# One step of a hybrid diffusion backbone: the values of four heads in one place, and when the output projection's buffers open

## The chip, the cores and the metric

The kernel runs on one core of a Trainium2 chip. The metric is the device time of one execution in microseconds, as the median of several runs. Names: PE is TensorE's matmuls and PEld its weight loads, DVE is VectorE, ACT ScalarE, POOL GpSimd, SP the engine whose queue issues the DMAs.

## The reference

Two identical layers. In each, one projection of the modulated input feeds four mixers; their gated outputs are joined and projected back, and a layer norm over the residual follows. The change touches mixer B (neighbourhood attention) and the output projection.

```
h   = x * (1 + scale) + shift
u   = h @ w_in + b_in
out = concat_g(mixer_g(u_g) * SiLU(gate_g)) @ w_out + b_out
x   = LayerNorm(alpha * x + gate * out)

# mixer B: 32 x 64 grid, 4 heads of 64; window of 8 rows x 16 columns, and all 256 context keys
s_loc = einsum('brchd,brjwhd->brhcjw', qg, kg) * scale
s_loc = where(col_in, s_loc + bias, NEG_INF)
s_ctx = einsum('brchd,bshd->brhcs', qg, k_ctx) * scale
p = softmax(concatenate([s_loc, s_ctx]))
o = einsum(p_loc, vg) + einsum(p_ctx, v_ctx)
```

There are 2048 latent tokens (32 rows of 64) and 128 context tokens of a new request, which attend only among themselves ("prompt" in the code). All is fp32; products that need it are split into a high and a low part and take three matmuls.

## The kernel before

Each layer has four stages: input projection, grouped-query attention, neighbourhood attention (phase3) and output projection (phase4). A stage opens pools of SBUF buffers on two stacks, one from the left and one from the right ("left" and "right" in `sub`), and closes them at its end. A buffer that comes to lie where an older one was can be written only when all readers of the old one are done, a DMA store among them. Order on each engine's queue is set by a planner, which takes instructions by readiness and program order; for this stage no order is written by hand. A queue runs strictly in the order that it was given.

**The neighbourhood attention** (L1213) works on 16 tiles, 8 groups i of four grid rows (in NAT_ORDER, 1 2 0 3 4 5 7 6) by two column halves e. Groups 0 and 7 are edge groups with a bias of their own, be, which a pool of one buffer holds in turn with the prompt's operands; the others use a resident bias bi. The loop at L1342 runs over pairs of heads, two steps a tile, as a pipeline of three: at step s the scores of pair s (L1266, L1267 into ps_d, two banks that phase 4 shares; then VectorE's L1272 adds the bias and takes the maximum, and ScalarE's L1276 the exponential), the transposes of pair s-1 (L1299; part 0 is copied to pT by VectorE at L1301, part 1 by ScalarE at L1303), and the values of pair s-2 (L1314, into ps_a, one bank; 5 key chunks a head in edge tiles and 6 in the others). With the second pair, `finish` broadcasts the denominators over TensorE (L1325), multiplies onto the gates gt (L1334) and, for e = 1, stores gt to the mixed output (L1337). pT has three buffers, one for each head in flight.

A value matmul has 64 output rows, so TensorE runs it in 128x64 form; scores, transposes and L1325 are in 128x128 form.

At step 8 `load_p4pre` fetches w_out in four chunks of 1 MB through the buffers of mx (two) and splits each: woh on ScalarE (L1453), wol on GpSimd (L1454). Steps 15 and 20 insert the prompt's attentions.

**The output projection** (L1464) takes 17 tiles t of 128 tokens. `load_mix(p)` loads two tiles' columns into mx, `prep(t)` (L1496) splits them into mhi (ScalarE, L1503, two halves) and mlo (GpSimd, L1507; for t = 0 VectorE makes the first half), in one set of buffers for even t and one for odd t (pmh). `main(t)` is 48 matmuls (L1536 to L1538, 2 column halves by 8 k by 3), its evacuation starts at L1529. Since open_p4pre opens the mx buffers and the even set before the attention runs, the planner may move load_mix and the first preps into the attention's last third, and it does.

Of the kernel before, what the change touches and what calls it, by code (L numbers as in the profile page):

```python
# [8 lines left out]
F32 = mybir.dt.float32  # L9
# [113 lines left out]
class Kern:  # L123
# [1081 lines left out]

    def phase3(self, l):
        P = lambda n, b: self.sub(f"p3{n}{l}", "p3", b, "right")
        self.open_p4pre(l)
        self.b2, self.be1 = P("b2", 2), P("be", 1)
        self._phase3(l)  # L1210
        self.close("p3")

    def _phase3(self, l):  # L1213
# [75 lines left out]
        def transp(i, e, h, part):  # L1289
            d = st[i, e]  # L1290
            p = d["p", h]
            ch = chunks(i, e)
            if part == 0:
                d["pT", h] = self.b3.tile([128, 6, 128], F32, tag="pT", name="pT")
            pT = d["pT", h]
            a, b = (0, len(ch) - 3) if part == 0 else (len(ch) - 3, len(ch))
            t = self.third((128, 4, 128))
            for c in range(a, b):
                nc.tensor.transpose(t[:, c - a, :], p[:, ch[c][0]:ch[c][0] + 128], self.id)  # L1299
            if part == 0:  # L1300
                nc.vector.tensor_copy(pT[:, a:b, :], t[:, :b - a, :])  # L1301
            else:
                nc.scalar.activation(pT[:, a:b, :], t[:, :b - a, :], AF.Copy)  # L1303
                d.pop(("p", h))

        def values(i, e, pr):
            d = st[i, e]
            if pr == 0:
                d["acc"] = self.bank("a", (128, 4, 128))
            ch = chunks(i, e)  # L1310
            for c, (_, vt, ti) in enumerate(ch):
                for hh in range(2):
                    h = pr * 2 + hh
                    nc.tensor.matmul(  # L1314
                        d["acc"][hh * 64:(hh + 1) * 64, pr, :], vt[:, ti, h * 64:(h + 1) * 64], d["pT", h][:, c, :],
                        start=(c == 0), stop=(c == len(ch) - 1),
                    )

        def finish(i, e):
            d = st.pop((i, e))  # L1320
            zb = self.b2.tile([128, 4, 64], F32, tag="zb", name="zb", bufs=1)
            nc.vector.reciprocal(d["z"], d["z"])
            nc.vector.tensor_copy(zb, d["z"].unsqueeze(2).to_broadcast([128, 4, 64]))
            for c in range(2):
                nc.tensor.matmul(  # L1325
                    d["acc"][:, 2 + c, :], zb[:, 2 * c:2 * c + 2, :].rearrange("p h d -> p (h d)"), self.id,
                    start=True, stop=True,
                )
            gt = gates[i]
            acc = d["acc"].rearrange("p a (r c) -> p a r c", r=4)  # L1330
            for x in (1, 0):
                for c in range(2):
                    g = gt[:, c, :].rearrange("p (r s c) -> p r s c", r=4, s=2)[:, :, e, :]
                    nc.vector.tensor_tensor(g, acc[:, 2 * x + c], g, op=ALU.mult)  # L1334
            if e == 1:
                c0 = NPR + i * 256
                nc.sync.dma_start(S["mix"][256:512, c0:c0 + 256].rearrange("(c p) t -> p c t", p=128), gates.pop(i))  # L1337
# [4 lines left out]
        for s in range(n + 2):  # L1342
            if s < n:
                i, e, pr = pairs[s]
                if pr == 0:
                    begin(i, e)
                scores(i, e, 2 * pr)
                scores(i, e, 2 * pr + 1)
                if pr == 1 and e == 1 and d_edge(i):
                    held.pop(("tile", i))  # L1350
                    load_edge()
            if 0 <= s - 1 < n:
                i, e, pr = pairs[s - 1]
                for hh in range(2):
                    transp(i, e, 2 * pr + hh, 0)
                    transp(i, e, 2 * pr + hh, 1)
            if 0 <= s - 2 < n:
                i, e, pr = pairs[s - 2]
                values(i, e, pr)
                if pr == 1:  # L1360
                    finish(i, e)
                    x = tiles.index((i, e))
                    if x + 2 < len(tiles):
                        self.load_nv(*tiles[x + 2])
            if s == 8:
                self.load_p4pre(l)
            if s in (15, 20):
                gqa = s == 20
                self.prompt_attn(l, gqa, *held.pop(("prompt", gqa)))
                load_edge()  # L1370
# [25 lines left out]
    def prompt_attn(self, l, gqa, q, k, v, gt):  # L1396

        nc, S = self.nc, self.S
        zb = self.b2.tile([128, 4, 64], F32, tag="zb", name="pzb", bufs=1)
        r0 = 768 if gqa else 256  # L1400
        s = self.bank("d", (128, 1024))
        for h in range(4):
            kh = h // 2 if gqa else h
            for i in range(2):
                nc.tensor.matmul(
                    s[:, h * 128:(h + 1) * 128], q[i][:, h, :].bitcast(F32R), k[:, kh, :].bitcast(F32R),
                    start=(i == 0), stop=(i == 1),
                )
        m = self.b2.tile([128, 8], F32, tag="pm", name="pm", bufs=1)
        s4 = s[:, 0:512].rearrange("p (h t) -> p h t", h=4)  # L1410
        nc.vector.tensor_reduce(m[:, 0:4], s4, axis=AX.X, op=ALU.max, negate=True)
        p = self.b3.tile([128, 4, 128], F32, tag="p", name="pp")
        z = m[:, 4:8]
        for h in range(4):
            nc.scalar.activation(p[:, h, :], s4[:, h, :], AF.Exp, bias=m[:, h:h + 1], accum_out=z[:, h:h + 1])
        t = self.third((128, 4, 128))
        for h in range(4):
            nc.tensor.transpose(t[:, h, :], p[:, h, :], self.id)
        pT = self.b3.tile([128, 4, 128], F32, tag="pT", name="ppT")
        nc.vector.tensor_copy(pT, t)  # L1420
        nc.vector.reciprocal(z, z)
        nc.vector.tensor_copy(zb, z.unsqueeze(2).to_broadcast([128, 4, 64]))
        acc = self.third((128, 4, 128))
        for h in range(4):
            kh = h // 2 if gqa else h
            nc.tensor.matmul(
                acc[(h % 2) * 64:(h % 2) * 64 + 64, h // 2, :], v[:, kh * 64:(kh + 1) * 64], pT[:, h, :],
                start=True, stop=True,
            )
        for c in range(2):  # L1430
            nc.tensor.matmul(
                acc[:, 2 + c, :], zb[:, 2 * c:2 * c + 2, :].rearrange("p h d -> p (h d)"), self.id, start=True, stop=True
            )
        nc.vector.tensor_tensor(gt, acc[:, 2:4, :], gt, op=ALU.mult)
        nc.vector.tensor_tensor(gt, acc[:, 0:2, :], gt, op=ALU.mult)
        nc.sync.dma_start(S["mix"][r0:r0 + 256, :NPR].rearrange("(c p) t -> p c t", p=128), gt)


    def open_p4pre(self, l):

        nc, A = self.nc, self.A
        c1 = self.sub(f"p4w{l}", "p4", 1, "left")
        self.pmx = self.sub(f"p4m{l}", "p4", 2, "left")
        self.pmh = [self.sub(f"p4h{l}", "p4", 1, "left"), None]
        self.woh = c1.tile([128, 8, 1024], F32R, name="woh")
        self.wol = c1.tile([128, 8, 1024], F32R, name="wol")

    def load_p4pre(self, l):
        nc, A = self.nc, self.A
        for k in range(0, 8, 2):  # L1450
            w = self.pmx.tile([128, 2, 1024], F32, tag="mx", name="wo")
            nc.sync.dma_start(w, A["w_out"][l][k * 128:(k + 2) * 128, :].rearrange("(k p) n -> p k n", p=128))
            nc.scalar.activation(self.woh[:, k:k + 2, :], w, AF.Copy)  # L1453
            nc.gpsimd.tensor_tensor(self.wol[:, k:k + 2, :], w, f32(self.woh[:, k:k + 2, :]), op=ALU.subtract)  # L1454

    def phase4(self, l):
        P = lambda n, b: self.sub(f"p4{n}{l}", "p4", b, "left")
        self.pmh[1], self.c1, self.b2 = P("h1", 1), P("c", 1), P("b2", 2)
        if l + 1 < self.depth:
            self.open_p1pre(l + 1)  # L1460
        self._phase4(l)
        self.close("p4")

    def _phase4(self, l):  # L1464
# [3 lines left out]
        mt = {}  # L1468

        def load_mix(p):  # L1470
            m = self.pmx.tile([128, 8, 256], F32, tag="mx", name="mx")
            n = min(256, T - p * 256)
            nc.sync.dma_start(m[:, :, :n], S["mix"][:, p * 256:p * 256 + n].rearrange("(k p) t -> p k t", p=128))
            mt[p] = m
# [262 lines left out]
```

## Time and profile before

| | us |
|---|---|
| median of 3 runs (lowest, highest) | 2886.11 (2882.16, 2894.56) |
| the profiled execution, its time | 2888.61 |
| its span from the first to the last instruction | 2886.7 |
| TensorE busy in the span | 2777.3 (96%) |
| VectorE busy | 1959.3 (68%) |
| GpSimd busy | 1100.5 (38%) |
| ScalarE busy | 1079.2 (37%) |
| mean granted TensorE clock | 0.984 |

Neighbourhood attention: about 1106 to 1287 us (layer 0) and 2526 to 2707 us (layer 1). Output projection: from there to 1495 and to the end; its first matmuls already run at 1266 and 2685.

How to read it: TensorE is busy nearly throughout, so shares of the whole span say little on a change in one stage. A table of busy times by stretch says which engine a stage is bound by; the waits name what an engine stood for; the timeline shows the queue around one wait. A busy TensorE includes the pitch that it loses at a change between forms. In a timeline row, equal instructions that follow one another are drawn together: start, time, engine, line, operation, operands, form, count, and in brackets the idle time before and what ended it.

### The profile page before, as it was taken

The numbers are of one execution on the slowest core, as the hardware profiler recorded it, in microseconds if no ns is written. First come the engines' busy times: TensorE is split into PE (matmuls) and PEld (weight loads), VectorE is DVE, ScalarE is ACT, GpSimd is POOL, SyncE is SP. The second block draws the span as 40 slices with busy tenths as digits, with TensorE's granted clock in tenths as the row PEclk, the third lists the DMA queues.
The fourth block names the chain that finished last, engine by engine and source line by source line (L and its number), as shares of the span: only waits on it lengthen the run. The fifth ranks groups of instructions, "written<-read, shape, count | busy, mean of one in ns | idle before, by whom it ended". The sixth has DMA issues, their size and how long they took to land. (4 is left out here: it accounts for less than half of the span.)

```text
span 2886.7 us, 45477 instructions
## 1 busy us (share of the span) xinstructions
PE 2777.3 (96%) x16960; PEld 2272.2 (79%) x16960; DVE 1959.3 (68%) x3503; ACT 1079.2 (37%) x1922; POOL 1100.5 (38%) x716
## 2 busy tenths in 40 slices
PE   7999999999999999999999899999999999999998
PEld 6988989999555556887779899999985555577887
DVE  2895246944478886749868963398436888676687
ACT  4233431333344445542222334313323444465210
POOL 3353420512466666014323534213215666730232
PEclk9999999999999999999999999999999999999999
DMA  9665775665361005646755556746555201076452
GB/s 311 216 209 185 212 251 178 194 201 158 89 146 35 21 21 155 166 137 225 235 180 176 175 182 189 239 149 219 148 157 121 71 24 35 8 206 177 135 168 103
DMA packets 384381, 447.80 MB, mean 155 GB/s; under 512 B 54432, under 2 KB 338592, under 8 KB 382368
## 3 DMA queue, kind: packets, MB, share of 16 engines
q1 hardware_dynamic: 384160, 444.89, 51.3%
q8 instruction: 134, 2.20, 0.3%
q14 instruction: 87, 0.71, 0.1%
HBM read 279.39 MB, written 165.39 MB: 154 GB/s over the span
## 5 line engine op out<-in xcount | busy, mean ns | idle before, releaser
L308 PE MATMUL ps_u<-hhi,whi 128*128 128x384 f32 (+1 forms) x1712 | 567.8, 335 | 11.0 <-ACT hhi L391 8.7
L309 PE MATMUL ps_u<-hlo,whi 128*128 128x384 f32 (+1 forms) x1712 | 567.2, 332 | 1.5 <-POOL hlo L393 0.7
L310 PE MATMUL ps_u<-hhi,wlo 128*128 128x384 f32 (+1 forms) x1712 | 565.8, 331 | 0.0
L1067 POOL TENSOR_TENSOR zp<-zp,e 128x1024 f32<-128x1024 f32 x160 | 388.5, 2428 | 217.7 <-ACT e L1049 214.1
L1049 ACT ACTIVATE e<-ps_d 128x1024 f32<-128x1024 f32 x288 | 292.0, 1024 | 361.1 <-PE ps_d L1047 328.7
L783 DVE SCALAR_TENSOR_TENSOR cacc<-cz,small,cacc 128x1166 f32<-128x1166 f32 (+1 forms) x240 | 356.7, 1486 | 3.5
L308 PEld LDWEIGHTS ps_u<-hhi,whi 128*128 128x128 f32 x1712 | 326.0, 191 | 20.3 <-ACT hhi L391 12.0
L309 PEld LDWEIGHTS ps_u<-hlo,whi 128*128 128x128 f32 x1712 | 326.9, 191 | 6.0 <-POOL hlo L393 2.6
L310 PEld LDWEIGHTS ps_u<-hhi,wlo 128*128 128x128 f32 x1712 | 326.7, 191 | 1.8 <-issue 1.0
L970 DVE TENSOR_REDUCE mx<-ps_s 128x1 f32<-128x512 f32 (+1 forms) x374 | 228.5, 631 | 122.1 <-PE ps_s L967 117.9
L1055 PE MATMUL ps_a<-e,gvv 128*64 128x512 f32 x1152 | 281.2, 609 | 0.0
L1507 POOL TENSOR_TENSOR mlo<-mx,mhi 128x512 fp32r<-128x512 f32 x66 | 110.8, 1698 | 417.4 <-ACT mhi L1503 417.4
L308 PE MATMUL ps_u<-whi,hhi 128*128 128x256 f32 x816 | 236.1, 289 | 0.0
L309 PE MATMUL ps_u<-wlo,hhi 128*128 128x256 f32 x816 | 234.9, 288 | 0.0
L310 PE MATMUL ps_u<-whi,hlo 128*128 128x256 f32 x816 | 234.8, 288 | 0.0
L433 POOL TENSOR_TENSOR wlo<-ws,whi 128x512 fp32r<-128x512 f32 x92 | 142.5, 1558 | 202.7 <-ACT whi L432 190.4
L1536 PE MATMUL ps_d<-woh,mhi 128*128 128x512 f32 x512 | 200.9, 392 | 0.0
L1537 PE MATMUL ps_d<-wol,mhi 128*128 128x512 f32 x512 | 200.7, 392 | 0.0
L1538 PE MATMUL ps_d<-woh,mlo 128*128 128x512 f32 x512 | 200.4, 391 | 0.0
L1029 PE MATMUL ps_d<-q,k 128*128 128x512 f32 x576 | 187.0, 407 | 2.6 <-ACT e L1049 2.0
L1047 PE MATMUL ps_d<-q,k 65*128 65x512 f32 x560 | 178.3, 399 | 0.2 <-ACT q L980 0.2
L1055 PEld LDWEIGHTS ps_a<-e,gvv 128*64 128x64 f32 x1152 | 71.7, 137 | 127.3 <-issue 125.0
(285 smaller groups left out, 5475.5 us busy)
## 6 DMA issues: line engine op xcount, KB each, us to landing
ws<-in_w_in SPq DMA_DIRECT2D x80, 256.0 KB
mw<-in_w_mod SPq DMA_DIRECT2D x32, 512.0 KB
nq<-s_nq SPq DMA_DIRECT2D x64, 256.0 KB
mx<-s_mix SPq DMA_DIRECT2D x16, 1024.0 KB
s_gate<-ev SPq DMA_DIRECT2D x80, 192.0 KB
s_qh<-qT SPq DMA_DIRECT2D x34, 256.0 KB
x<-in_x SPq DMA_DIRECT2D x17, 512.0 KB
s_xT<-xo SPq DMA_DIRECT2D x17, 512.0 KB
```

Source lines behind the costliest of these rows:

```text
L308: mm(p, ah, bh, start=(k == 0), stop=False)
L309: mm(p, ah, bl, start=False, stop=False)
L310: return mm(p, al, bh, start=False, stop=(k == 7))
L783: nc.vector.scalar_tensor_tensor(acc[:, c, :n], z[:, k:k + n], cw[:, c, k:k + 1], acc[:, c, :n], op0=ALU.mult, op1=ALU.add)
L970: r = nc.vector.tensor_reduce(mx[:, h, i:i + 1], p[:, :n], axis=AX.X, op=ALU.max)
L1029: nc.tensor.matmul(s[:, kv * 512:(kv + 1) * 512], k1[kv][:, j * 128:(j + 1) * 128], q1[:, 2 * kv:2 * kv + 2, :].rearrange("p h t -> p (h t ...
L1049: nc.scalar.activation(e, s, AF.Exp)
L1055: nc.tensor.matmul(acc[kv * 64:(kv + 1) * 64, :], vv[:, j, kv * 64:(kv + 1) * 64], e[:, kv * 512:(kv + 1) * 512], start=(j == 0), stop=(j ...
L1067: nc.gpsimd.tensor_tensor(zp, zp, e, op=ALU.add)
L1536: nc.tensor.matmul(o, hi[:, k, :], woh[:, k, ns], start=(k == 0), stop=False)
L1537: nc.tensor.matmul(o, hi[:, k, :], wol[:, k, ns], start=False, stop=False)
L1538: nc.tensor.matmul(o, lo[:, k, :], woh[:, k, ns], start=False, stop=(k == 7))
```

## The change

Three edits. In the loop of the neighbourhood attention, `values` of both pairs of a tile is called at the second pair's step, so that of the first pair comes one step later. pT moves to a pool of its own with six buffers instead of three, opened ahead of the output projection's early buffers. And these early buffers shrink to the weights and one mx buffer, through which w_out is loaded; the second mx buffer and the even mhi/mlo set are opened with phase 4, on top of the left-hand stack, at the addresses they had.

```diff
@@ phase3
         P = lambda n, b: self.sub(f"p3{n}{l}", "p3", b, "right")
+        self.b3t = P("t", 6)
         self.open_p4pre(l)
@@ transp, and likewise ppT in prompt_attn
-                d["pT", h] = self.b3.tile([128, 6, 128], F32, tag="pT", name="pT")
+                d["pT", h] = self.b3t.tile([128, 6, 128], F32, tag="pT", name="pT")
@@ _phase3, the loop
                 i, e, pr = pairs[s - 2]
-                values(i, e, pr)
                 if pr == 1:
+
+                    values(i, e, 0)
+                    values(i, e, 1)
                     finish(i, e)
@@ open_p4pre
-        self.pmx = self.sub(f"p4m{l}", "p4", 2, "left")
-        self.pmh = [self.sub(f"p4h{l}", "p4", 1, "left"), None]
+        self.pmx = [self.sub(f"p4m{l}", "p4", 1, "left")]
@@ load_p4pre
-            w = self.pmx.tile([128, 2, 1024], F32, tag="mx", name="wo")
+            w = self.pmx[0].tile([128, 2, 1024], F32, tag="mx", name="wo")
@@ phase4
-        self.pmh[1], self.c1, self.b2 = P("h1", 1), P("c", 1), P("b2", 2)
+        self.pmx.append(P("m1", 1))
+        self.pmh = [P("h", 1), P("h1", 1)]
+        self.c1, self.b2 = P("c", 1), P("b2", 2)
@@ load_mix
-            m = self.pmx.tile([128, 8, 256], F32, tag="mx", name="mx")
+            m = self.pmx[p % 2].tile([128, 8, 256], F32, tag="mx", name="mx")
```

## Rows read from the trace of the kernel before

**Rows 1.** Busy by stretch: PE, PEld, DVE, ACT, POOL, clock, DMA, GB/s.

```profile
1106.00:1287.00 181.00, 173.17 (x1539) 144.88 (x1538) 120.73 (x372) 100.19 (x220) 29.88 (x12) 0.99 0.61 167
1230.00:1240.00 10.00, 6.78 (x53) 6.04 (x52) 4.82 (x17) 5.63 (x13) 1.28 (x1) 0.83 1.11 282
2650.00:2660.00 10.00, 7.22 (x58) 6.04 (x59) 5.74 (x17) 5.29 (x12) 1.26 (x1) 0.83 1.02 252
1340.00:1370.00 30.00, 26.69 (x126) 21.77 (x125) 29.23 (x42) 10.93 (x22) 15.39 (x11) 1.00 0.71 227
2780.00:2820.00 40.00, 40.00 (x178) 33.14 (x177) 32.72 (x37) 5.80 (x12) 13.89 (x8) 1.00 0.47 158
```

**Rows 2.** Waits of PE, 1106 to 1287: total us, times, longest.

```profile
PE ps_d L1266 <- DVE m L1272: 4.4, 3, 3.2
```

**Rows 3.** Timeline of ACT around prep(0) and prep(1), both layers.

```profile
1232.05 0.63 ACT L1503 ACTIVATE mhi<-mx 128x512 fp32r<-128x512 f32 x1 [4.43 <-DMA mx<-s_mix]
...
1250.04 1.15 ACT L1503 ACTIVATE mhi<-mx 128x512 fp32r<-128x512 f32 x2 [0.36 <-DVE m L1272]
...
2650.43 1.15 ACT L1503 ACTIVATE mhi<-mx 128x512 fp32r<-128x512 f32 x2 [3.10 <-issue]
```

**Rows 4.** Timeline of PE: three tiles' L1325, layer 0.

```profile
1228.68 0.71 PE L1325 MATMUL ps_a<-small,zb 128*128 128x128 f32 x4
...
1242.91 0.71 PE L1325 MATMUL ps_a<-small,zb 128*128 128x128 f32 x4
...
1251.11 0.71 PE L1325 MATMUL ps_a<-small,zb 128*128 128x128 f32 x4
```

**Rows 5.** Timeline of PE: 16 value matmuls, undisturbed and after the stall.

```profile
1208.88 1.09 PE L1314 MATMUL ps_a<-pT,nv 128*64 128x128 f32 x16
...
1236.16 1.97 PE L1314 MATMUL ps_a<-pT,nv 128*64 128x128 f32 x16
```

**Rows 6.** Groups of PE, 1265.7 to 1286.15; then timelines of PE, DVE, SP, POOL.

```profile
L1536 PE MATMUL ps_d<-woh,mhi 128*128 128x512 f32 x19 | 7.5, 396 | 0.0
...
1286.16 0.71 PE L1325 MATMUL ps_a<-small,zb 128*128 128x128 f32 x4
...
1286.91 0.88 DVE L1334 TENSOR_TENSOR gt<-ps_a,gt 128x128 f32<-128x128 f32 x4 [6.75 <-PE ps_a L1325]
...
1245.11 0.38 SPq L1337 DMA_DIRECT2D s_mix<-gt  x1
1247.26 0.38 SPq L1243 DMA_DIRECT2D gt<-s_gate  x1
...
2651.71 1.26 POOL L1507 TENSOR_TENSOR mlo<-mx,mhi 128x512 fp32r<-128x512 f32 x1 [81.18 <-ACT mhi L1503]
```

**Rows 7.** Waits of ACT; group of L1454 (ns min/median/max, first and last start), 1106 to 1287.

```profile
ACT woh L1453 <- DMA wo<-in_w_out: 5.3, 3, 1.9
...
L1454 POOL TENSOR_TENSOR wol<-wo,woh x4: 4575/4584/4633, 1125.6 to 1144.3; 128x2048 fp32r<-128x2048 f32 x4
```

**Rows 8.** Timeline of PE: runs of value matmuls of one edge tile and what follows them.

```profile
1245.70 0.88 PE L1314 MATMUL ps_a<-pT,nv 128*64 128x128 f32 x12
...
1247.16 0.44 PE L1299 MATMUL ps_s<-small,p 128*128 128x128 f32 x2
...
1249.02 0.66 PE L1314 MATMUL ps_a<-pT,nv 128*64 128x128 f32 x8
1249.61 0.55 PE L1299 MATMUL ps_s<-small,p 128*128 128x128 f32 x3
...
1250.31 0.32 PE L1314 MATMUL ps_a<-pT,nv 128*64 128x128 f32 x1
```

**Rows 9.** Waits of PEld in either layer's attention, and of DVE in layer 0's.

```profile
PEld ps_a L1314 <- issue: 8.6, 50, 0.4
...
PEld ps_a L1314 <- issue: 9.3, 52, 0.4
...
DVE pT L1301 <- PE ps_a L1314: 12.0, 10, 5.3
```

More of the change, by code (lines that the diff above doesn't have):

```diff
@@ L1418, in prompt_attn @@
             nc.tensor.transpose(t[:, h, :], p[:, h, :], self.id)
-        pT = self.b3.tile([128, 4, 128], F32, tag="pT", name="ppT")
+        pT = self.b3t.tile([128, 4, 128], F32, tag="pT", name="ppT")
         nc.vector.tensor_copy(pT, t)
```

## The prediction

> **What bounds the kernel now.** I read the table by stretch first, since the change touches only the third stage of each layer and the first microseconds of the fourth. In the neighbourhood attention of layer 0 TensorE is busy 173.17 of 181.00 us, while VectorE, ScalarE and GpSimd have 121, 100 and 30 us of work [rows 1]. So TensorE is the bound there, and what it loses is some 8 us of idle time, time at a lower clock, and whatever its own instructions waste. In layer 1's output projection it never idles; in layer 0's it gives way to VectorE for a while (26.69 of 30 us, VectorE 29.23) [rows 1]. That matters below: a delay at the start of that stage reaches the end of layer 1 whole, and that of layer 0 perhaps in part.
>
> Next the waits of TensorE in the stage. The largest by far in layer 0 is a score matmul that waited 3.2 us for VectorE's L1272 [rows 2]. The ten-microsecond stretches around it and its twin in layer 1 show TensorE at 6.78 and 7.22 us of work and a granted clock of 0.83 [rows 1]. VectorE is only the last link: ScalarE's queue shows mhi, the first step of the output projection's prep(0), standing 4.43 us for the load of mx with the exponentials queued behind it; layer 1 has the same place with 3.10 us [rows 3]. The second prep, at 1250.04, waits 0.36 us [rows 3]. The price: from one tile's L1325 to the next takes 14.23 us across the stall (1228.68 to 1242.91) and 8.20 us for the next tile, also an edge tile (1242.91 to 1251.11) [rows 4]. So the stall costs 6.0 us in layer 0: 3.22 idle, and a mean clock of 0.83 over 10 us, which is 3.4 us at the lower of the two levels (1.2 GHz) or 1.7 us of work, the rest lost around them. After its 3.22 us of idling TensorE ran 16 value matmuls in 1.97 us, against 1.09 us at 2.4 GHz [rows 5].
>
> **Part 1, the pools.** From the shapes, the second mx buffer (8 KB a partition) and mhi/mlo of even t (8 KB) leave the room shared with this stage, and three more pT (9 KB) enter it. The right-hand stack therefore reaches down to about byte 100,200, and the phase 4 buffers, whose addresses stay, now lie under it: mhi/mlo of t=0 under the edge bias be; mhi of t=1 under both gt buffers; mlo of t=1 under the second gt, z, zb and the first pT. Two consequences.
>
> First, prep(0) can no longer run at 1232. It has to wait until the last scores that read be, those of tile row 7, are done, and this is where prep(1) runs today: 1250.04 [rows 3]. By then mx has landed 18 us before. prep(0) takes prep(1)'s place at the same work (two mhi of 0.6 us on ScalarE), and that work shows a stall of 0.36 us there. So the 4.43 us stall goes: a gain of 6.0 us in layer 0 and, with 0.44 us less idle in its window, 5.6 us in layer 1, together **-11.6**. Its floor is the idle time of the two windows alone, 3.2 + 2.8 = 6.0.
>
> Second, prep(1) must wait for the last store of gt. Today main(0) and main(1) fill the stage's end: L1536 runs 19 times between 1265.7 and the last L1325 at 1286.16 [rows 6], 16 of these are main(0)'s, so main(1) has three, and with them two each of L1537 and L1538: 7 matmuls of main(1), and nothing idles. After the change those 7 can't be there. At 0.23 us each L1325 comes at 1284.55. The gt products start 0.75 us later and take 0.88 [rows 6]: 1286.2. A load that waits for a gt store's landing starts 2.15 us after its issue (1245.11, 1247.26) [rows 6]: 1288.3. Then mhi 0.6 and the first half of mlo 1.26 us on GpSimd [rows 6]: 1290.2. main(1)'s third matmul needs that mlo, so TensorE sits from 1285.1 to 1290.2 but for two matmuls, and main(1) ends after 46 more (1300.8) rather than 41 right behind today's L1325 (1286.6 to 1296.1): 4.7 us. After that much idling I add the same 1.7 us of low clock as above: 6.4 us in layer 1. In layer 0 some may be absorbed where VectorE is the late one: I take 5.0. Together **+11.4**, bounds 0 (the store's wait hidden, both times) and 16 (8 each, if the second mlo half is waited for too).
>
> Smaller: the loads of w_out have one buffer rather than two. ScalarE waits 5.3 us for them now in layer 0, three times, and GpSimd takes 4.58 us for a chunk [rows 7]. A single buffer lets the next load be issued only after GpSimd's step; with the flight and ScalarE's step ahead of it I estimate 10 us for a chunk, about twice GpSimd's, and 40 for four: done at about 1165, needed at 1266. What can reach TensorE is a ScalarE wait in front of exponentials. Bounds -2 (loads that come singly land sooner, so the 5.3 shrinks) and +3; I take **+1.4**, nearest to half of the present waits. And be now lies under buffers of the stage before, so its load waits for that stage's last store and the gt loads queue behind it on SP; both are needed later than they would land. **+0.5**, bounds 0 and 1. load_mix(1) and load_mix(2) start later too, but two and four tiles of 11 us ahead of need: 0.
>
> **Part 2, the values.** In the program both halves of a tile's values now stand together, one step later for the first half. What it may give: a value matmul is in 128x64 form, its neighbours in 128x128, and each change of form costs. An unbroken run of 22 takes 1.46 us (1245.70 to 1247.16), one of 8 takes 0.59, one of 10 takes 0.80 [rows 8]. From 8 to 22 is 0.87 for 14 matmuls, 0.062 each, so one run of 40 would take 1.46 + 18 x 0.062 = 2.58 against 2.85 for the three: 0.13 for each run saved, and with the pitch into the run (0.2 rather than 0.11 between transposes) about 0.25. There are some 50 runs in layer 0 and 52 in layer 1, counted by the weight loads that stood for no other reason (8.6 and 9.3 us) [rows 9]. With one run a tile, and a few broken ones, they would be 36: 66 saved by 0.25, **-17**.
>
> What TensorE shows against it: the queue isn't in program order. Values already run as soon as their pT is copied, in the gaps in which the next scores wait for VectorE. That is what splits a tile into 22, 8 and 10, and the program moves only a priority. One cause of splitting does go: with three pT buffers the copy of head 3 waits for the first pair's values (VectorE 12.0 us, ten times in layer 0 [rows 9]), and with six it needn't. But that VectorE time is off the critical path, and with no wait the second pair's first values are merely ready sooner. Below nothing: the accumulator has one buffer, and if the first pair's values slide one step later the tile's L1325 and the next tile's values come in a lump, with short runs filling in; ten more runs a layer would be +5. So -17 to +5, and I take **0**, since the row of today's runs shows the split at readiness and not at the program's grouping.
>
> The Trainium skill, page "TensorEngine Tiling (Array Packing)", section Key Properties, says that changing the tiling mode drains the engine, and the trace agrees: the pitch grows at both ends of a run. By that rule alone, taken with the new grouping, the sum would hold the -17, which is the first rival below.
>
> **The sum.** -11.6 + 11.4 + 1.4 + 0.5 + 0 = +1.7 us. The profiled run took 2888.61 us, so 2890.3 by it; that run is 2.5 us above the median of the three (2886.11), so I forecast **2888 us**.
>
> **The rivals.**
> - *The values really run together* (-17 on top): 2888 - 17 = 2871. For it: the cause of the 1, 6 and 5 split of the second pair, the pT wait, is gone. Against it: the first split, into 20 + 2, has another cause, the wait for scores. Chance 0.20.
> - *The tail hides itself*: main(1)'s delay is absorbed by VectorE's stretch in layer 0 and the low clock stays away, so the tail costs 0 to 5 rather than 11.4: about 2879. For it: VectorE is nearly full early in that stage; against it: layer 1 has no such stretch. Chance 0.17. Part of it, with a few runs saved, is over 0.5% faster.
> - *Slower: the stall only moves.* mhi(0) is queued on ScalarE where be is expected free; if the scores of tile row 7 are later than planned, ScalarE stands before the exponentials as it does now, and the -11.6 is gone while the tail is paid: 2888 + 11.6 = 2900, and 2902 with a few more runs. It decides from the point where mhi waits some 4 us again; the 0.36 us at 1250.04 speaks against it. Chance 0.13.
> - *The change doesn't do what it says*: as many runs as before. That is inside my forecast; it costs only what the pools bring.
>
> **How the numbers follow.** Forecast 0.50, rivals 0.20, 0.17, 0.13. 0.5% is about what a measurement here can tell from no change: 14.4 us, so 2871.7 and 2900.5. Faster: the first rival (0.20, it lies on the bound and a little less than all of it counts) and a part of the second: 0.24. Slower: most of the third: 0.10. Same: 0.66. The range takes in the first rival's centre and the third's: 2868 to 2901. Inside the forecast alone it would be 2880 to 2897.
>
> **What would show it.** In the changed profile: ScalarE's mhi with no wait for mx, first at about 1248 to 1251 (step 1); TensorE at 9 tenths and clock 1.00 through that stretch; a new idle of some 5 us on TensorE before L1538 of main(1), right after the last L1325, released by GpSimd's mlo (step 2); four loads of w_out some 10 us apart; the count of weight loads L1314 that stood for "issue", near 50 if I am right and near 18 if the first rival is. I am wrong if that count falls by half, if no idle follows the last L1325, or if the stall at mhi stays.

## The result and the profile after

The changed kernel is slower: 2913.89 us (2902.08 to 2921.25, six runs) against 2886.78 (2877.12 to 2894.56, six runs), a ratio of 1.0091 with a 95% interval of 1.0075 to 1.0107, so some 26 us. The forecast was 2888 with a range up to 2901.

The profiled execution of the changed kernel took 2921.25 us, 7.4 above its median, and just 7.4 us of its surplus lie in stages that the change doesn't touch: from the last L1540 of layer 0 to the first score of layer 1 there are 1046.0 us, 1038.6 between the same points before. The rest is in the touched stages, from the first score to the last L1540: 11.2 us in layer 0 and 16.6 in layer 1 (the first score of layer 0 came 2.4 us earlier).

The table by stretch of the changed kernel (columns as in [rows 1]; first the two layers' attention, then two places in them, the place of the old stall, and the 20 us after the attention of layer 0):

```profile
1104.00:1284.00 180.00, 170.01 (x1499) 138.20 (x1499) 118.52 (x371) 98.81 (x216) 24.54 (x8) 0.99 0.59 159
2543.00:2724.00 181.00, 172.84 (x1496) 139.06 (x1496) 119.31 (x371) 98.89 (x216) 24.25 (x8) 0.97 0.57 158
1134.00:1144.00 10.00, 9.72 (x77) 8.16 (x77) 6.20 (x20) 6.52 (x16) 3.62 (x1) 0.83 0.44 121
2623.00:2633.00 10.00, 10.00 (x76) 7.51 (x76) 5.04 (x16) 4.27 (x9) 0.00 (x0) 0.84 0.46 108
1230.00:1240.00 10.00, 10.00 (x105) 8.69 (x101) 7.73 (x26) 5.60 (x13) 0.00 (x0) 1.00 0.76 232
1284.00:1294.00 10.00, 6.74 (x32) 5.27 (x30) 2.11 (x5) 1.61 (x3) 4.02 (x3) 1.00 0.83 245
1294.00:1304.00 10.00, 9.78 (x36) 7.92 (x37) 6.04 (x8) 2.27 (x4) 6.73 (x4) 0.83 0.86 305
```

Two things went as forecast: at 1230 to 1240 TensorE is busy throughout at full clock (6.78 us and 0.83 before, [rows 1]), and behind the attention there is a new idle with the lower clock after it (3.5 us, released by ScalarE's mhi, where some 5 us and GpSimd's mlo were forecast). The attention itself did not gain. TensorE is busy 170.01 us in it, 3.2 less than before [rows 1], but it now holds far fewer matmuls of the output projection. In the groups of TensorE up to the last L1326 of layer 0 these are 7 + 7 + 6 = 20, where 55 stood before [rows 6]:

```profile
L1540 PE MATMUL ps_d<-woh,mhi 128*128 128x512 f32 x7 | 2.9, 419 | 0.0
L1541 PE MATMUL ps_d<-wol,mhi 128*128 128x512 f32 x7 | 2.9, 416 | 0.0
L1542 PE MATMUL ps_d<-woh,mlo 128*128 128x512 f32 x6 | 2.5, 412 | 0.0
```

At 0.23 us each (an estimate, the pitch of output matmuls in an undisturbed row), the attention's own part of the busy time is 170.0 - 4.6 = 165.4 us against 173.2 - 12.7 = 160.5 before: 4.9 us more for the same instructions, and 6.9 in layer 1. Of these 6.9 some 3.4 us are not pitch but lower clock: the mean clock over the 181 us of layer 1's attention is 0.97, where it was 0.99 (worked out from the clock's own rows, 5.1 us lost and 1.7). The pitch alone has thus grown by some 8.4 us in the two layers. Idle time, within the attention, rose from 7.8 to 10.0 and from 6.1 to 8.2 us although the stall of 3.2 and 2.8 us is gone. So the 16.6 us of layer 1 come to 3.5 us of pitch, 3.4 of lower clock and 2.1 of idle in the attention, and 3.9 of idle and 1.7 of lower clock behind it; 2.0 us are not placed. The new waits with their lower clock cost more there than the pitch. The longest waits of TensorE there (total, times, longest; first layer 0, then layer 1) are new ones but for the one for m, which stands at the start of the attention before the change too:

```profile
PE ps_a L1315 <- ACT pT L1304: 2.2, 1, 2.2
PE ps_a L1315 <- DMA nv<-s_nv: 2.0, 1, 2.0
PE ps_a L1315 <- DVE m L1276: 1.8, 1, 1.8
...
PE ps_a L1315 <- DMA nv<-s_nv: 2.8, 1, 2.8
PE ps_s L1300 <- ACT p L1277: 2.7, 1, 2.7
```

Counted in the trace from the first score to the last L1326, the value matmuls stand in 68 and 72 unbroken runs in the two layers, 56 and 55 before. (The expectations below also count runs in the order of TensorE's queue as built, 113 before and 144 changed, some of whose instructions have no record.) The sign that the forecast named, weight loads that stood for "issue", rose as well, from 50 and 52 [rows 9] to 56 and 64:

```profile
PEld ps_a L1315 <- issue: 12.3, 56, 2.2
...
PEld ps_a L1315 <- issue: 15.2, 64, 3.0
```

### The profile page after: what moved, and what is told of

Same layout as the page of the kernel before. It is cut to its first block, busy times and chain, and to the rows that moved or that the text cites. A ratio compares the mean times of both kernels' runs of the same rounds, so it can differ in the third digit from the quotient of the medians.

```text
span 2919.5 us, 45384 instructions
## 1 busy us (share of the span) xinstructions
PE 2796.1 (96%) x16960; PEld 2275.0 (78%) x16960; DVE 1944.4 (67%) x3503; ACT 1082.7 (37%) x1922; POOL 1099.6 (38%) x716
## 5 line engine op out<-in xcount | busy, mean ns | idle before, releaser
L1540 PE MATMUL ps_d<-woh,mhi 128*128 128x512 f32 x512 | 202.6, 396 | 7.4 <-ACT mhi L1507 7.4
```

What stands on the lines that cost most here:

```text
L1540: nc.tensor.matmul(o, hi[:, k, :], woh[:, k, ns], start=(k == 0), stop=False)
```

## The experiments

Times are medians; a difference is taken from the ratios, 0.1% being 2.9 us. The changed kernel stands at +0.91%. A difference between two kernels has an interval of some 5 to 8 us either way, worked out from those of the two ratios.

**One thing given back at a time.** The place of the calls:

```diff
                 i, e, pr = pairs[s - 2]
+                values(i, e, pr)
                 if pr == 1:
-                    values(i, e, 0)
-                    values(i, e, 1)
```

> The changed kernel with its pools, but each pair's values called at its own step again, as before the change. The changed kernel took 2913.9 us (before 2886.8). In its attention the value matmuls come in 68 and 72 unbroken runs in the two layers, 56 and 55 before, and the pitches around them grew by some 12 us in all, about 0.4 us for a run more. Theory 1 (the new place of the calls makes less than half of the additional runs, the rest comes with the pools): 2907 to 2910 us, some 60 to 64 runs a layer. Theory 2 (the place of the calls is what costs): runs back at 55 a layer and 2895 to 2900 us. Theory 3 (the place is indifferent, the planner orders by readiness): runs as in the changed kernel, 2912 to 2916.

2904.4 us, ratio 1.0052 (1.0034 to 1.0070), 64 runs in each layer: 11 us back, a little more than theory 1 said, and far from all.

The second buffer for w_out:

```diff
+        self.wox = self.sub(f"p4x{l}", "p4x", 1, "left")
...
-        for k in range(0, 8, 2):
-            w = self.pmx[0].tile([128, 2, 1024], F32, tag="mx", name="wo")
+        for k, j in ((0, 2), (2, 1), (3, 2), (5, 1), (6, 2)):
+            w = (self.pmx[0] if j == 2 else self.wox).tile([128, j, 1024], F32, ...)
```

> The changed kernel with a second, 4 KB buffer for the loads of w_out during the attention (five chunks of 1, 0.5, 1, 0.5 and 1 MB in turn). In the changed kernel ScalarE stands 10.9 and 7.0 us for these loads (5.3 and 0 before). Theory 1 (this single buffer makes ScalarE stand with exponentials behind it, TensorE then idles and runs at the lower clock; together 3 to 5 us a layer): 2904 to 2909 us, with waits for w_out at 6 us or less in both layers. Theory 2 (hidden, as forecast: at most 3 us in all): 2911 to 2915.

2905.4 us, 1.0066 (1.0043 to 1.0090): 7 us back, as theory 1 said, but with an interval of -1 to 15 us it is not clear of no gain. ScalarE's waits for w_out in the changed kernel, layer 0 and layer 1:

```profile
ACT woh L1455 <- DMA wo<-in_w_out: 10.9, 3, 6.5
...
ACT woh L1455 <- DMA wo<-in_w_out: 7.0, 2, 5.8
```

and with the second buffer:

```profile
ACT woh L1457 <- DMA wo<-in_w_out: 5.4, 3, 3.4
...
ACT woh L1457 <- DMA wo<-in_w_out: 3.6, 1, 3.6
```

TensorE's waits for nv are gone here, too: idle in the attention is 5.0 and 5.2 us, not 10.0 and 8.2.

The order of phase 4's pools, odd mhi/mlo set first:

```diff
-        self.pmx.append(P("m1", 1))
-        self.pmh = [P("h", 1), P("h1", 1)]
+        h1, h = P("h1", 1), P("h", 1)
+        self.pmh = [h, h1]
+        self.pmx.append(P("m1", 1))
```

> The changed kernel with the three pools opened by phase 4 in another order: the odd mhi/mlo/x set first, then the even set, then the second mx buffer, so that both mhi/mlo sets lie under the edge bias and only the second mx buffer, not needed before t = 2, lies under the gates' buffers. Theory 1 (the tail costs what its idle of 3.5 and 3.9 us, the low clock behind it and VectorE's slack say, 3.2 + 5.7 us): 2903 to 2907 us, no idle of TensorE after the last L1326, and main(1) in part ahead of it again. Theory 2 (that idle is covered by something else that is late, such as the gate's load for the first evacuation): 2911 to 2915.

2902.0 us, 1.0046 (1.0031 to 1.0061): 13 us back, a little more than theory 1 (2903 to 2907), and no idle of TensorE over 0.1 us in the 20 us after the attention of layer 0, 1.1 us in layer 1.

**The first rival made true.** The call's place didn't hold the values together; an order on TensorE does:

```diff
+                    with self.tc.issue_after(st["lastT"]):
                         values(i, e, 0)
                         values(i, e, 1)
```

(lastT is the transpose traced last.)

> The changed kernel with one order added: on TensorE a tile's values stand behind the transposes traced before them (the first pair of the next tile), so that all 40 or 48 really run together: 38 runs in the whole kernel, 140 in the changed one. Theory 1 (a run costs 0.25 us, as forecast for the first rival, or 0.4 as the changed trace suggests): 26 to 42 us less, 2872 to 2888. Theory 2 (broken runs fill gaps in which the scores wait for VectorE; held together they leave these gaps open): TensorE's idle in the attention rises by 10 us a layer or more and the time stays at 2905 or above.

2921.0 us, 1.0117 (1.0101 to 1.0133): theory 2. Both layers' attention by stretch:

```profile
1106.00:1292.00 186.00, 168.05 (x1527) 144.71 (x1527) 115.00 (x373) 97.59 (x216) 23.18 (x8) 0.96 0.57 154
2544.00:2726.00 182.00, 166.06 (x1526) 142.75 (x1525) 120.30 (x372) 96.97 (x216) 23.61 (x8) 0.97 0.58 158
```

The waits of TensorE in layer 0's attention, and in the 30 us after it:

```profile
PE ps_d L1267 <- DVE m L1273: 7.2, 16, 2.6
PE ps_s L1300 <- ACT p L1277: 4.4, 2, 2.2
...
PE ps_d L1542 <- ACT mhi L1509: 9.2, 1, 9.2
```

The runs fell to 17 a layer, and the busy time without the 45 output matmuls to 168.1 - 10.4 = 157.7 us, 7.7 under the changed kernel, though more of it ran at the lower clock. So the saving that the forecast priced is real: 0.15 us a run, 0.25 with the 5 us of additional lower clock counted in. But TensorE is now idle 17.9 and 15.9 us in the attention: scores wait for VectorE 16 times, once 2.6 us and 0.3 us on the mean of the others, in gaps that the broken runs probably used to fill. Behind the attention it is idle 9.2 us in layer 0, where the changed kernel has 3.5. The first rival's price was about right and its kernel loses all the same.

**What costs by itself, in the kernel before.** One buffer for w_out:

```diff
-        self.pmx = self.sub(f"p4m{l}", "p4", 2, "left")
+        self.pmx = [self.sub(f"p4m{x}{l}", "p4", 1, "left") for x in range(2)]
...
-            w = self.pmx.tile([128, 2, 1024], F32, tag="mx", name="wo")
+            w = self.pmx[0].tile([128, 2, 1024], F32, tag="mx", name="wo")
...
-            m = self.pmx.tile([128, 8, 256], F32, tag="mx", name="mx")
+            m = self.pmx[p % 2].tile([128, 8, 256], F32, tag="mx", name="mx")
```

> The kernel before with one alteration: the loads of w_out go through one of the two mx buffers only. All else (places of the values, three pT, both mhi/mlo sets) is as before. Giving a second buffer back to the changed kernel was worth 7 us (2905.4 against 2913.9). Theory 1 (the single buffer costs by itself: ScalarE waits behind w_out, w_out's issue waits for GpSimd on SP, and TensorE loses 3 to 4 us a layer): 2893 to 2897 us, ScalarE's wait for w_out at 7 us or more a layer. Theory 2 (it costs only together with the later values and six pT): 2886 to 2890.

2892.9 us, 1.0017 (1.0002 to 1.0032): 5 us, just clear of none. It costs by itself, though ScalarE's waits for w_out are only 1.7 and 4.2 us, so theory 1 has about its time and not its mechanism; runs rose to 59 and 60.

**Things given back together.** Whole tiles with both other returns:

> All values of a tile held together by an order on TensorE (2921.0 us in the changed kernel, 38 runs, TensorE's idle 17.4 and 15.5 us in the attention and 9.2 and 9.8 us behind it), now with the second buffer for w_out and with the odd mhi/mlo set opened first. Theory 1 (the idle behind the attention goes whole, with its low clock of some 3 us a layer, and 7 us with w_out's buffer): 2921 - 25 - 7 = 2889, range 2885 to 2894, no better than the kernel before, since the scores' waits for VectorE (7 and 5 us) stay open. Theory 2 (what remains after both is the saving of 70 runs at 0.25 us, 17 us): 2866 to 2874.

2912.3 us, 1.0090 (1.0075 to 1.0105): worse than theory 1. Behind the attention 5.9 and 6.5 us of idle remain, now because the second mx buffer, which this order of the pools lays under the gates, is loaded late; the waits for VectorE stay.

All three returned (pairs as before, second buffer for w_out, odd set first):

> Of the change only six pT, and the early preps taken out of the attention's middle, are left: values pair by pair, a second buffer for w_out, the odd mhi/mlo set first. The three single returns were worth 11, 7 and 13 us by ratio (31 in all, of 26 that the change costs). Theory 1 (they add up): 2887 + 26 - 31 = 2882 us, 2878 to 2885, below the kernel before because ScalarE's stand for mx is gone. Theory 2 (they overlap, and six pT by themselves bring some ten more runs a layer): 2888 to 2896.

2893.2 us, 1.0030 (1.0016 to 1.0044): theory 2. The three single returns of 11, 7 and 13 us are worth 17.6 together, and what remains of the change, with no stall at mx, is still 9 us above the kernel before, with 64 and 65 runs.

The same, with each pair's values held together by the order used above:

> As the run with three things back, and on TensorE the values of each pair stand behind the transposes traced before them, so that 20 or 24 run together: 68 runs in the whole kernel rather than 133, with two places a tile, not one, at which TensorE leaves the scores and transposes. Theory 1 (a run costs 0.22 us, from the values' pitch sums of 46 and 44 us in 17 runs a layer against 56 and 57 in 68 and 72, and the gaps stay filled): 10 to 15 us less than the run with three things back. Theory 2 (the gaps in which the scores wait for VectorE open): TensorE's idle in the attention rises over 12 us a layer and the time is the same or longer.

2897.5 us, 1.0039 (1.0024 to 1.0055): theory 2 by its idle, 13.6 and 13.4 us where the run with three things back has 4.6 and 6.3, at 32 runs a layer. The attention's own busy time is some 10 us a layer lower. Fewer runs again, less pitch, and no gain.

**The number of pT.** First with three pT, twice as large so that addresses stay, in the kernel with three things back and in the changed kernel:

```diff
-        self.b3t = P("t", 6)
+        self.b3t = P("t", 3)
...
-                d["pT", h] = self.b3t.tile([128, 6, 128], F32, tag="pT", name="pT")
+                d["pT", h] = self.b3t.tile([128, 12, 128], F32, tag="pT", name="pT")
```

> The run with three things back (pair by pair, second buffer for w_out, odd set first: 2893.2 us, 0.3% over the kernel before, 64 and 65 runs of value matmuls a layer) with three pT instead of six; each is made twice as large, so that every address stays. Theory 1 (with six pT the second pair's values become ready head by head and break into more runs; three are a brake that keeps them together): about 5 runs a layer fewer and 3 to 5 us less, 2888 to 2890. Theory 2 (the number of pT is indifferent, the runs come from elsewhere): 2892 to 2894.

> The changed kernel with three pT of twice the size instead of six, all else as changed (addresses, one buffer for w_out, values of both pairs at the second step). Theory 1 (the brake is undone by the later place of the values itself: both pairs are then released together and compete with the scores in the planner): runs about as in the changed kernel, 2910 to 2914 us. Theory 2 (six pT are what makes the additional runs): 2900 to 2906 us and under 62 runs a layer.

2906.1 us, 1.0065 (1.0052 to 1.0078), and 2922.8 us, 1.0120 (1.0104 to 1.0136): both slower than with six, against every theory. The runs of value matmuls did not fall back to 56 and 55: they are 64 and 58 in the first kernel (64 and 65 with six) and 72 and 64 in the second (68 and 72 with six), although VectorE's copies of pT wait for the first pair's values again, and longer than before the change (12.0 us, [rows 9]). Layer 0's attention in the two kernels:

```profile
DVE pT L1303 <- PE ps_a L1316: 16.0, 21, 5.4
```

```profile
DVE pT L1302 <- PE ps_a L1315: 21.4, 24, 4.7
```

What makes them slower is mostly behind the attention. With three pT the planner again runs main(0) and part of main(1) inside it (55 matmuls in the first kernel, 38 and 48 in the second), so nothing is left to cover the next wait on a gates' buffer. In the first, main(2) stood 8.27 us, since its mx could only be loaded after the gates' store. Its timeline on PE, then on ACT:

```profile
1302.92 0.79 PE L1541 MATMUL ps_d<-woh,mhi 128*128 128x512 f32 x1 [8.27 <-ACT mhi L1508]
```

```profile
1302.24 2.19 ACT L1508 ACTIVATE mhi<-mx 128x512 fp32r<-128x512 f32 x4 [2.65 <-DMA mx<-s_mix]
```

Then a kernel without that wait, the kernel before with four pT, and the even set opened with phase 4 to make room:

```diff
+        self.b3t = P("t", 4)
...
-        self.pmh = [self.sub(f"p4h{l}", "p4", 1, "left"), None]
...
-        self.pmh[1], self.c1, self.b2 = P("h1", 1), P("c", 1), P("b2", 2)
+        self.pmh = [P("h", 1), P("h1", 1)]
+        self.c1, self.b2 = P("c", 1), P("b2", 2)
```

(pT and ppT are taken from b3t, as in the change.)

> The kernel before with four pT instead of three, and the even mhi/mlo set opened with phase 4 to make room, which also puts prep(0) behind the edge bias, as the change does; two mx buffers, odd set and values pair by pair as before. With three pT in the same code the order on TensorE is that of the kernel before, 113 runs in all; with four it is 137. Theory 1 (pT is a brake that keeps values together, and each run more costs 0.25 to 0.45 us): 6 to 11 us for 24 runs less 6.6 for the stand that goes, 2886 to 2893, and TensorE's pitches of values and scores 3 to 6 us a layer above those of the kernel before. Theory 2 (runs are indifferent): 2880 to 2882, as with prep(0) later alone.

2896.3 us, 1.0032 (1.0020 to 1.0045), with no stall at mx: a little above theory 1's range. In the trace 68 and 65 runs; by stretch:

```profile
1105.00:1285.00 180.00, 171.48 (x1508) 139.56 (x1505) 119.86 (x375) 99.16 (x218) 26.32 (x10) 0.99 0.60 158
2527.00:2708.00 181.00, 171.58 (x1503) 139.97 (x1504) 122.56 (x375) 99.96 (x218) 26.02 (x10) 0.97 0.57 156
```

Without its 20 output matmuls the attention's busy time is 166.9 and 167.0 us, 6.4 and 5.7 above the kernel before (3.4 of the 5.7 are more of the lower clock). So a fourth pT, with the later even set, is enough for as many runs in layer 0 as the changed kernel has. What it costs is less plain: from the first score to the last output matmul the profile is 1.4 us longer than before in layer 0, and 9.5 in layer 1, where some 7 of the 9.5 are a wait of TensorE for nv and the 3.4 us of lower clock:

```profile
PE ps_a L1315 <- DMA nv<-s_nv: 3.6, 1, 3.6
```

This kernel also runs 35 output matmuls fewer inside the attention; three pT in the same pools (113 runs in the built order against 137, by the expectation) were not measured.

**The gain by itself.** The kernel before with prep(0) later on ScalarE, and the same with the second mx load later too:

```diff
+                if t == 0:
+                    with self.tc.issue_after(self.lateexp):
+                        r = nc.scalar.activation(hi[:, k], m[:, k, ms], AF.Copy)
...
+            if p == 1:
+                with self.tc.issue_after(self.lastnv):
+                    nc.sync.dma_start(m[:, :, :n], src)
```

(The first part is the first kernel; lateexp is the last exponential of group 7's first half, lastnv the nv load traced last.)

> The kernel before with one order added: prep(0)'s two steps on ScalarE stand behind the last exponential of tile row 7's first half, some 12 us after mx has landed. Nothing else is altered. It measures the gain of the forecast by itself. Theory 1 (the stand for mx costs 6.0 and 5.6 us): 11 to 12 us under the kernel before, 2876 to 2879, no idle of TensorE of 1 us or more at that place. Theory 2 (only the idle time of 3.2 and 2.8 us counts, the low clock behind it comes anyway): 5 to 7 us, 2882 to 2884. Theory 3 (the later prep pushes something else late): no gain, 2887 to 2890.

> The kernel before with prep(0) later (2881.0 us, 0.23% under the kernel before, where 11 to 12 us had been forecast for the stand that it removes) and, in addition, the load of the second mx (token pair 1) behind the last load of nv on SP. With prep(0) later alone, TensorE stood 2.9 us in layer 0 for nv, whose loads were issued just behind the 2 MB of both mx loads. Theory 1 (part of the gain is given back there): that wait is gone and the time 2 to 4 us lower, 2877 to 2879. Theory 2 (the nv wait is one of several small ones that come and go with any new order): 2880 to 2882, some other wait in its place.

2881.0 us, 0.9977 (0.9967 to 0.9987), and 2877.8 us, 0.9975 (0.9959 to 0.9990): both beat the kernel before by 7 us, not 11 to 12, and the changed one by more. For the first that is theory 2 by its size, though in layer 1 the lower clock went as well (0.99 before, 1.00 here). Layer 0 waits in other places, as its waits of TensorE show:

```profile
PE ps_a L1316 <- DMA nv<-s_nv: 2.9, 1, 2.9
PE ps_s L1301 <- ACT pT L1305: 2.4, 1, 2.4
```

In the second that nv wait is gone, and the ratio is the same within its interval: theory 2. Half of the forecast gain is not found in either. Nor do the profiles place it: from the first score to the last output matmul the first kernel is 1.1 and 1.5 us shorter than the kernel before, the second 9.5 shorter in layer 0 and 1.8 longer in layer 1, one execution each.

**The end of the attention.** The changed kernel with the constants' loads behind the last store of gt:

```diff
+        with self.tc.issue_after(self.laststore):
             load_gate(0)
             nc.sync.dma_start(lng, A["ln_g_bc"][l])
             nc.sync.dma_start(lnb, A["ln_b_bc"][l])
```

> The changed kernel with the loads of gb, bo, lng and lnb (half a megabyte each) behind the last store of gt on SP. In the changed kernel they are issued 0.5 to 1.9 us ahead of that store, and mhi of prep(1), which waits for its landing, starts 7.9 us after its issue, not 2.15. Theory 1 (the store stands in the DMA queues behind these loads): mhi of prep(1) starts 2 to 3 us after the store's issue, TensorE's idle of 3.5 and 3.9 us behind the last L1326 goes with its low clock, 2902 to 2906 us. Theory 2 (the landing is late by itself, or the evacuation then waits for gb): 2911 to 2915.

2900.4 us, 1.0046 (1.0033 to 1.0059): 13 us back, theory 1 and more. The timeline of the changed kernel on SP, then on ACT and PE:

```profile
1283.79 0.35 SPq L1487 DMA_DIRECT2D gb<-s_g  x1
1284.19 0.42 SPq L1489 DMA_DIRECT2D bo<-in_b_out_bc  x1
1284.65 0.43 SPq L1495 DMA_DIRECT2D lng<-in_ln_g_bc  x1
1285.13 0.43 SPq L1496 DMA_DIRECT2D lnb<-in_ln_b_bc  x1
1285.66 0.47 SPq L1338 DMA_DIRECT2D s_mix<-gt  x1
```

```profile
1290.60 1.15 ACT L1507 ACTIVATE mhi<-mx 128x512 fp32r<-128x512 f32 x2 [9.94 <-PE ps_d L1541]
1293.54 1.15 ACT L1507 ACTIVATE mhi<-mx 128x512 fp32r<-128x512 f32 x2 [1.79 <-issue]
...
1294.22 0.50 PE L1540 MATMUL ps_d<-woh,mhi 128*128 128x512 f32 x1 [3.49 <-ACT mhi L1507]
```

and of this one, SP and then ACT:

```profile
1283.85 0.38 SPq L1338 DMA_DIRECT2D s_mix<-gt  x1
1284.33 0.40 SPq L1488 DMA_DIRECT2D gb<-s_g  x1
...
1286.17 1.15 ACT L1509 ACTIVATE mhi<-mx 128x512 fp32r<-128x512 f32 x2 [6.98 <-DMA s_mix<-gt]
```

The store and the mhi that waits for it lie 7.9 us apart in the changed kernel and 2.3 us apart here. The loads of constants, whose buffers the change frees earlier, had gone ahead of the store on SP; with the order turned round, the store's landing is early again.

## Why the prediction was wrong

**The stall at mx: right place, half the size.** prep(0) moved behind the edge bias and waits 0.5 us there; the stall is gone. The term of -11.6 measures -6.6 (the interval of that run is 3.8 to 9.5 us). It was priced as the time between two L1325 across the stall less the time of the next tile, 14.23 - 8.20 [rows 4]. That probably counts as lost what other engines had caught up during the stall; no run shows it. The floor that the forecast named, the idle of the two windows (6.0), was nearer. What covers the rest is open: in layer 0 a wait for nv took 2.9 us of it in one order and not in the next, at no difference in time.

**The end of the attention: right sum, wrong steps.** Forecast +11.4; the two kernels that remove it are 13 us faster. Both steps on the way failed. The wait behind the store was taken as 2.15 us from a store with nothing ahead of it [rows 6], where the changed order sends 2 MB of loads first. And main(0) was thought to fill the attention's end as before; 28 of its matmuls now come behind it and cover some 6.4 us. The two errors cancel in part, so that the sum came out is luck.

**w_out through one buffer: forecast +1.4, measured 5 to 7.** The chain was called early enough, and it is, though its chunks come 13 to 17 us apart, not 10, and it is done by 1183, not 1165, in layer 0. The step that failed is the last one, what reaches TensorE: the bound of 3 us was one ScalarE wait. ScalarE's waits for w_out did rise, from 5.3 and 0 us to 10.9 and 7.0. That they carry the cost is not shown: the kernel before with one buffer costs 5 us with waits of 1.7 and 4.2, and the kernel with the calls given back is 11 us faster than the changed one with waits of 16.0 and 7.9. w_out's issue also shares SP with the nv loads, for which TensorE waits 2.0 and 2.8 us in the changed kernel; how the cost arises stays open.

**The values: forecast 0, measured a loss.** This is the step that made the range too narrow. Part 2 was set at 0, as many runs as before, with +5 as its bound. Measured are 12 and 17 runs more, some 8.4 us of pitch for them, and the waits and the lower clock of the new order on top. The price of a run was about right: 0.25 us forecast, 0.4 in layer 0 (4.9 us for 12) and 0.2 in layer 1 (3.5 for 17). Their number was wrong, and the waits that a new order brings were put at nothing. The later calls are a part of it that is shown: giving them back alone is worth 11 us.

The Trainium skill ("TensorEngine Tiling (Array Packing)", Key Properties) states that changing the tiling mode drains the engine. These runs agree: 17 runs rather than 68 gave 7.7 us of busy time back.

The other part is the number of pT, and it is shown only in part. The forecast saw the wait of pT's copies for the first pair's values (12.0 us, ten times [rows 9]) and dismissed it as VectorE time off the critical path. It is off the path, but it may be a brake: with three pT, head 3's copy can't run before the first pair's values are done. In the traces with four or six pT that wait is absent, and the runs are more where no order holds them together. A typical inner tile shows the new break between its two pairs: runs of 26, 12 and 10 before, of 24, 2, 12 and 10 after. Against the brake as the whole cause stand the two kernels with three pT, which have the wait and 64 and 58, 72 and 64 runs. So the number matters in the built order of the kernel before (113 runs with three, 137 with four), but what else in the moved pools breaks the runs stays open. The run with four pT stands at +0.32% with the stall gone, where the stall alone gives -0.23%; the 0.55% or 16 us (11 to 21) between them hold the additional runs, but also the wait for nv with its lower clock and whatever the later even set costs. It is no price of a pT.

**The sum as it is now.** -6.6 for the stall, 16 from there to the kernel with four pT, 17.6 for the three other parts together, from the run with three things back to the changed kernel: 27, where 26 was measured. It closes because the run with three things back (+0.30%) and the run with four pT (+0.32%) agree, though they are built from opposite ends. How the 16 divides between runs and waits is not settled.

**The rivals.** The first, whole runs, did not happen in the changed kernel (68 and 72, not 18), and forced, it loses in idle what it saves in runs, or more. The second, a tail that hides itself, did not happen. The third had the right sign for a wrong reason: no stall at mhi. The case that came true, more runs and several waits at once, stood only in the bounds, where it was cut off at +5.

## What to carry to other kernels

A buffer that an engine waits for can also set the order of another engine's work; before more buffers are given, look at what the wait orders, not only whom it delays. A new order brings waits of its own, and with lower clock behind them they cost more in layer 1 than the changes of form did. When pools move, list for each new wait on a DMA what may now be issued ahead of it on the same queue, since its price is not that of the same DMA in an empty queue. And a saving on TensorE's changes of form is only had if nothing was filling gaps with the broken runs.

## What the runs showed of the hardware

With a store of 256 KB that had nothing ahead, the load that waited for its landing was issued about 2.2 us after it; behind four loads of half a megabyte issued in the 1.9 us before it, such a store held its waiter for 7.9 us, and 2.3 us when these loads went behind it. In the changed kernel the lower clock came in portions of much the same size: 10 us at a mean of 0.83 or 0.84 behind TensorE's waits of 2.2 us (1133), 2.8 us (layer 1, 2622) and 3.5 us (1294), 1.6 to 1.7 us of work each, as behind the 3.22 us before [rows 1]. The length of the wait does not tell it alone: no lower clock is recorded behind the 2.0 us for nv at 1183, and a wait of 2.1 us for m at the start of layer 1's attention has it in the changed kernel (2553) and not before the change (2537).
